# Rope scores of an attention stage on 64 array rows, four banks in one group per tile

## The chip, the core and the metric

One core of a Trainium2 chip runs the whole program. Its engines are TensorE (PE; its weight loads are listed as PEld), VectorE (DVE), ScalarE (ACT), GpSimd (POOL) and SyncE (SP), which here issues the DMAs. The metric is the device time of one execution in microseconds (us), the median of three. Times inside the program come from one profiled execution.

## The reference, cut to what matters

The program is one layer of an encoder: RMS norm and an input projection, an mLSTM head group, an attention head group, an output projection, a gated MLP and a gated per-layer embedding, on 2048 positions of width 1024. The change lies in the attention group (4 heads, 128 plain and 64 rope columns for each query and key) and at a few places before it:

```python
def mla_group(c_q, c_kv, k_rope_pre, q_norm_g, w_uq, kv_norm_g, w_ukv, cos, sin):
    q = (rms_norm(c_q, q_norm_g) @ w_uq).reshape(bsz, s, MLA_HEADS, QK_NOPE + QK_ROPE)
    q_nope, q_rope = q[..., :QK_NOPE], q[..., QK_NOPE:]
    q_rope = apply_rope(q_rope, cos[:, None, :], sin[:, None, :])
...
    scale = (QK_NOPE + QK_ROPE) ** -0.5
...
    def attend(blk):
        qn, qr = blk
        sc = (jnp.einsum('bqhd,bkhd->bhqk', qn, k_nope)
              + jnp.einsum('bqhr,bkr->bhqk', qr, k_rope))
        pr = jax.nn.softmax(sc.astype(jnp.float32) * scale, axis=-1)
        return jnp.einsum('bhqk,bkhd->bqhd', pr.astype(v.dtype), v)
```

## The kernel before, in words

Products keep float32 accuracy by splitting each operand into a high part, rounded to the reduced format fp32r, and a low part, the rest (`split`, L120 and L123). A product is then three matmuls: low by high, high by low, high by high (`mm3`, L133).

`in_proj` projects 128 rows of x at a time. `ssq_x` squares a tile of x on ACT, adds on DVE and sums over partitions with two matmuls by a column of ones (L237); POOL takes the power that gives the row's norm factor. `rest` (the columns for gates, query, key and rope) uses that factor one step later. `q_up`, run as side work between matmuls of a later part of the projection, makes the queries: DVE forms four rope products from PSUM (L607 to L610), the rotated result is turned and split, and one DRAM tensor, `q_d`, takes the plain part and, in its second plane, the rope part: its high half in rows 0 to 63, its low half in rows 64 to 127. Rope keys are the same for all heads. `split_kr` holds them twice over, in rows 0 to 63 and 64 to 127: `kr2` is the high part, `krl` the low part.

The attention stage runs over 64 tiles (4 heads by 16 tiles of 128 queries). A tile's scores against 2048 keys fill four PSUM banks of 128 x 512, and there are four such banks, so a bank has to be read by the exponential of one tile before the next tile's matmuls may use it. `score_bank` makes one bank with five matmuls (L918 to L922); two of them carry the rope part, L919 (`qr` by `krl`) and L921 (`qr` by `kr2`), where the 128 rows of `qr` hold the high and the low part of the query. DVE then takes the bank's maximum (L923). `soft` takes the maximum of the four, and a second instruction multiplies it by minus the scale (L934, L935). `expo` exponentiates a bank on ACT with that bias, the scale, and the row's sum (L941); after the fourth bank DVE adds the sums and inverts them (L946, L947). `transp` transposes a bank of exponentials (L981) into one of two banks and splits it, high on ACT, low on DVE. `pv` multiplies by the values for a pair of tiles, half the keys at a time (L993, L994); after the second half ACT copies (L997), DVE adds (L998), and two DMAs store the result (L1000). Queries come a pair of tiles ahead: `load_q` by one DMA (L900), three tiles before they are used, and `split_q`.

The order in which a tile's steps are written is a string:

```python
        order = "s0 E1 . s1 E2 . . t0 . s2 . E3 . t1 . s3 . . X e0 t2 . . t3 V . .".split()
```

Here s is a score bank of the next tile, E and e exponentials (E of the current tile, e0 the first of the next), t a transposition of the current tile, X `soft`, V half a value product, and at each point a step of side work may go, which is the mLSTM stage. A planner at compile time then fixes the order on each engine from that order and its own estimate of when operands are ready; `keep_in_program_order` pins one instruction behind the one written before it on its engine. On the chip each engine works through its fixed order. The output sums (`osums`, DVE) prepare weights of the later output projection beside attention.

Of the kernel before, what the change touches and what calls it, by code (L numbers as in the profile page):

```python
# [60 lines left out]
class Block:  # L61
# [114 lines left out]
    def in_proj(self):  # L176
# [51 lines left out]
        def ssq_x(st, x_t):  # L228
# [5 lines left out]
            nc.vector.tensor_tensor(ss[:, 0:2], ss[:, 0:2], ss[:, 2:4], op=ALU.add)  # L234
            ps = self.pml.tile([P, 4], F32, name="ssp", tag="ml")
            for i in range(2):
                nc.tensor.matmul(ps, ss[:, i], ones, start=i == 0, stop=i == 1)  # L237
# [65 lines left out]
        for st in range(NT + LAG_X):  # L303
# [9 lines left out]
            if 0 <= st - 1 < NT:  # L313
                ssq_x(st - 1, xq.pop(st - 1))
            if 0 <= st - LAG_X < NT:
                nq[st - LAG_X] = rest(st - LAG_X)
            if 0 <= st - LAG_X - LAG_R < NT:
                turn_rest(st - LAG_X - LAG_R, nq.pop(st - LAG_X - LAG_R))
# [174 lines left out]
    def split_kr(self, raws):  # L493

        self.kr2, self.krl = [self.at(f"x{14 + i}", [P, S], F32R, f"kr{i}") for i in range(2)]
        for c in range(4):
            sl = slice(c * 512, (c + 1) * 512)
            self.split(raws[c // 2][:, (c % 2) * 512:(c % 2) * 512 + 512], self.kr2[:, sl], self.krl[:, sl])
# [68 lines left out]
    def q_up(self):  # L567
# [16 lines left out]
        for c in range(8):  # L584
# [12 lines left out]
            for t in range(2):  # L597
# [9 lines left out]
                nc.vector.tensor_tensor(tt[:, 0], x1, cos, op=ALU.mult)  # L607
                nc.vector.tensor_tensor(tt[:, 1], x2, sin, op=ALU.mult)
                nc.vector.tensor_tensor(tt[:, 2], x2, cos, op=ALU.mult)
                nc.vector.tensor_tensor(tt[:, 3], x1, sin, op=ALU.mult)  # L610
# [9 lines left out]
                nc.scalar.copy(o[:, 2 * t:2 * t + 2], ps)  # L620
# [270 lines left out]
    def attend_begin(self):  # L891
# [6 lines left out]
        def load_q(h, pr):  # L898
            q = self.at(f"w{4 - pr % 2}", [P, 2, 256], F32R, "q_t")
            nc.sync.dma_start(_f(q), self.q_d[h, pr])  # L900
            qv[h, pr] = q

        def split_q(h, pr):
# [4 lines left out]
            qv[h, pr] = qs[:, 0], qs[:, 1], q[:, 1]  # L908
# [4 lines left out]
        def score_bank(s, kb):  # L913
            h, qt = s.h, s.qt
            qh, ql, qr = [t[:, (qt % 2) * P:(qt % 2) * P + P] for t in qv[h, qt // 2]]
            ks = slice(kb * 512, (kb + 1) * 512)
            ps = self.bank()
            mm(ps, ql, kh[:, ks], start=True, stop=False)  # L918
            mm(ps, qr, self.krl[:, ks], start=False, stop=False)  # L919
            mm(ps, qh, kl[:, ks], start=False, stop=False)  # L920
            mm(ps, qr, self.kr2[:, ks], start=False, stop=False)  # L921
            mm(ps, qh, kh[:, ks], start=False, stop=True)  # L922
            nc.vector.tensor_reduce(s.mx[:, kb:kb + 1], ps, axis=AX.X, op=ALU.max)  # L923
            s.banks.append(ps)
# [7 lines left out]
        def soft(s):  # L932
            s.nm = self.stat(1, "nm")
            nc.vector.tensor_reduce(s.nm, s.mx, axis=AX.X, op=ALU.max)  # L934
# [1141 lines left out]
```

## Time and profile before

| what | us |
|---|---|
| runs | 2884.54, 2886.15, 2884.79 (median 2884.79) |
| profiled execution | 2882.77, of which its span 2881.0 |
| granted TensorE clock, mean | 0.999 of full speed |
| attention stage | from about 494 to about 1217 of the span |

A row of the groups gives line, engine, operation, tile names (out<-in), shapes and count, then busy us and the mean ns of one, then the idle time of the engine just before and what ended it. In the timeline a row gives start, duration, engine, line and what ran; a name ending in x4 merges four in a row. The duration of a matmul is its latency through a pipeline, so consecutive ones overlap and the distance between starts is what one costs.

### The profile page before, as it was taken

The page shows a single profiled execution, that of the slowest core. Times are in us where ns is not written, and L with a number is a line of the kernel's source. Part 1 is how long each engine was busy: PE and PEld are TensorE (multiplying, and loading weights), DVE is VectorE, ACT ScalarE, POOL GpSimd, SP SyncE. Part 2 cuts the span into 40 slices and gives each one's busy share as a digit, 9 for nine tenths or more (in the row PEclk, how much of TensorE's full clock was granted, in tenths as well). Part 3 has the DMA queues.
Part 4 walks back from the last instruction along what each step waited for, and adds up shares of the span by engine and source line. Part 5 has one row for each costly group of instructions (what it writes and reads, how often), then busy time and mean ns, then how long its engine had stood idle before and what let it go on. Part 6 is the DMA issues. An engine that isn't in the chain of part 4 may idle for free.

```text
span 2881.0 us, 40250 instructions
## 1 busy us (share of the span) xinstructions
PE 2848.1 (99%) x14110; PEld 2387.4 (83%) x14110; DVE 2044.2 (71%) x3790; ACT 1508.0 (52%) x3006; POOL 220.6 (8%) x331
## 2 busy tenths in 40 slices
PE   8999999999999999999999999999999999999998
PEld 7888888888888888788888888888888888888787
DVE  7521555877777777776777877867777867676777
ACT  7311544656666566655755555655556333254665
POOL 3100000000000010034300000000000000002012
PEclk9999999999999999999999999999999999999999
DMA  6512545653333333378845544657766767576864
GB/s 194 129 59 68 168 121 173 211 175 114 105 112 98 98 112 111 125 246 274 273 140 177 194 167 149 217 183 239 235 230 208 238 193 246 165 265 204 287 203 163
DMA packets 408314, 508.94 MB, mean 177 GB/s; under 512 B 34080, under 2 KB 271664, under 8 KB 408112
## 3 DMA queue, kind: packets, MB, share of 16 engines
q1 hardware_dynamic: 408112, 506.37, 55.0%
q8 instruction: 111, 1.82, 0.2%
q14 instruction: 91, 0.75, 0.1%
HBM read 324.16 MB, written 182.12 MB: 176 GB/s over the span
## 4 chain that ended last, share of the span: by engine, by line
PE 88%; DVE 4%; issue 2%; DMA 2%; ACT 2%; POOL 1%; SPq 0%; POOLq 0%; ACTq 0%; DVEq 0%
PE fy L1440 21%; PE fz L1440 14%; PE fx L1440 14%; PE bk L133 14%; PE ppv L993 3%; PE tb L981 3%; PE bk L918 2%; PE bk L922 2%; PE bk L920 2%; PE bk L919 2%; PE bk L921 2%; PE ppv L994 2%; PE fs L133 2%; PE gb L133 1%; PE mb L856 1%
## 5 line engine op out<-in xcount | busy, mean ns | idle before, releaser
L1440 PE MATMUL fz<-op,fw 128*128 128x512 f32 x1968 | 478.2, 391 | 3.5 <-ACT fw L120 3.0
L1440 PE MATMUL fx<-op,fw 128*128 128x512 f32 x1968 | 475.8, 390 | 0.0
L1440 PE MATMUL fy<-op,fw 128*128 128x512 f32 x1968 | 474.8, 390 | 0.0
L1440 PEld LDWEIGHTS fz<-op,fw 128*128 128x128 f32 x1968 | 367.1, 188 | 82.1 <-ACT fw L120 4.6
L1440 PEld LDWEIGHTS fy<-op,fw 128*128 128x128 f32 x1968 | 368.6, 188 | 76.7 <-ACT fy L1553 0.4
L1440 PEld LDWEIGHTS fx<-op,fw 128*128 128x128 f32 x1968 | 368.2, 188 | 76.0
L1440 PE MATMUL fy<-op,fwd 128*128 128x512 f32 (+1 forms) x984 | 238.0, 390 | 0.5 <-DVE uv L1425 0.5
L120 ACT CAST pt<-tb 128x512 fp32r<-128x512 f32 x256 | 147.4, 587 | 166.8 <-PE tb L981 165.9
L133 PE MATMUL bk<-wsp,xh 128*128 128x512 f32 (+1 forms) x768 | 234.3, 386 | 0.0
L1440 PEld LDWEIGHTS fy<-op,fwd 128*128 128x128 f32 x984 | 182.6, 188 | 38.4 <-DVE uv L1425 0.9
L923 DVE TENSOR_REDUCE mx<-bk 128x1 f32<-128x512 f32 x256 | 174.4, 683 | 42.5 <-PE bk L922 41.4
L123 DVE TENSOR_TENSOR pt<-tb,pt 128x512 fp32r<-128x512 f32 x256 | 174.0, 683 | 30.0 <-ACT pt L120 28.5
L941 ACT ACTIVATE pe<-bk,nm 128x512 f32<-128x512 f32 x256 | 174.8, 696 | 35.6 <-DVE nm L935 33.6
L993 PE MATMUL ppv<-pt,kv 128*128 128x512 f32 x512 | 188.9, 407 | 0.5 <-DVE pt L123 0.5
L133 PEld LDWEIGHTS bk<-wsp,xh 128*128 128x128 f32 x768 | 145.3, 189 | 25.2
L133 PE MATMUL bk<-wsp,xl 128*128 128x512 f32 (+1 forms) x384 | 150.6, 392 | 7.7 <-DVE xl L123 7.7
L133 PE MATMUL bk<-xh,wqk 128*128 128x512 f32 x480 | 157.1, 393 | 0.0
L981 PE MATMUL tb<-ident,pe 128*128 128x128 f32 x1024 | 150.8, 273 | 3.9 <-DVE pt L123 3.3
L994 PE MATMUL ppv<-pt,kv 128*128 128x256 f32 x512 | 145.0, 283 | 0.0
L981 PEld LDWEIGHTS tb<-ident,pe 128*128 128x128 f32 x1024 | 121.9, 140 | 24.6 <-DVE pt L123 6.3
L120 ACT CAST fw<-hraw 128x1024 fp32r<-128x1024 f32 (+1 forms) x72 | 70.2, 981 | 116.1 <-PE fx L1440 58.9
L120 ACT CAST op<-opr 128x512 fp32r<-128x512 f32 x165 | 96.3, 620 | 60.2 <-DMA opr<-tw_d 13.3
(366 smaller groups left out, 5172.7 us busy)
## 6 DMA issues: line engine op xcount, KB each, us to landing
fwr<-in_w_up SPq DMA_DIRECT2D x66, 512.0 KB, 5.1
fh<-h_d SPq DMA_DIRECT2D x48, 512.0 KB, 3.7
h_d<-fh SPq DMA_DIRECT2D x48, 512.0 KB, 4.5
s_d<-fwr SPq DMA_DIRECT2D x44, 512.0 KB, 2.9
fws<-s_d SPq DMA_DIRECT2D x44, 512.0 KB, 3.6
rw<-row_d SPq DMA_DIRECT2D x32, 512.0 KB, 5.4
tw_d<-tsum SPq DMA_DIRECT2D x60, 256.0 KB, 5.2
opr<-tw_d SPq DMA_DIRECT2D x60, 256.0 KB, 4.8
```

The lines of the kernel that those rows point to most:

```text
L120: nc.scalar.copy(hi, src)
L123: (sub or nc.vector).tensor_tensor(lo, src, _f(hi), op=ALU.subtract)
L133: mm = lambda *a, **k: self.nc.tensor.matmul(*a, **k, skip_group_check=more)
L918: mm(ps, ql, kh[:, ks], start=True, stop=False)
L919: mm(ps, qr, self.krl[:, ks], start=False, stop=False)
L920: mm(ps, qh, kl[:, ks], start=False, stop=False)
L923: nc.vector.tensor_reduce(s.mx[:, kb:kb + 1], ps, axis=AX.X, op=ALU.max)
L941: nc.scalar.activation(s.pe[:, kb % 2], s.banks[kb], AF.Exp, bias=s.nm, scale=ASCALE, accum_out=s.rs[:, kb:kb + 1])
L981: nc.tensor.transpose(t[:, j, :], s.p[kb][:, j * P:(j + 1) * P], self.ident)
L993: mm(w.ps, vh[:, ks], pts[kb][:, j], start=kt == 0, stop=False, skip_group_check=True)
L994: mm(w.ps[:, 0], vl[:, ks], pts[kb][:, j, 0], start=False, stop=kt == NT - 1, skip_group_check=True)
L1440: nc.tensor.matmul(out, a[:, k * P:(k + 1) * P], parts[lo][:, cols], start=first, stop=lo == 1 and k == last, skip_group_check=more)
```

## The change

The rope part by high parts (L921) is taken out of the banks' own steps. In the fourth score step, after its first matmul, four matmuls on 64 array rows follow one another, one for each bank: banks 0 and 2 on rows 0 to 63, banks 1 and 3 on rows 64 to 127. For the odd ones the high query part is loaded a second time, into rows 64 to 127 of a third plane of the query tile. The product of the query's low part with the key's high part moves into L919: rows 64 to 127 of `krl` now hold the key itself, rounded. The maxima of banks 0 to 2 are taken after the group. The scale goes into the queries where they are made, and the maximum comes out negated.

Beside this, `rowsum` and the end of the value product (`pv_end`) become steps of their own, later in the order and pinned; the row sums of x (`rms_x`) move behind `rest`; and the output sums are pinned in written order.

```diff
@@ -232,9 +232,14 @@
             nc.vector.tensor_tensor(ss[:, 0:2], ss[:, 0:2], ss[:, 2:4], op=ALU.add)
+            return ss
+
+        def rms_x(st, ss):
             ps = self.pml.tile([P, 4], F32, name="ssp", tag="ml")
             for i in range(2):
-                nc.tensor.matmul(ps, ss[:, i], ones, start=i == 0, stop=i == 1)
+                m = nc.tensor.matmul(ps, ss[:, i], ones, start=i == 0, stop=i == 1)
+                if i == 0:
+                    self.tc.keep_in_program_order(m)
             t = self.stat(1, "rsm")
@@ -310,10 +315,11 @@
                 split_x(st, xq[st])
-            if 0 <= st - 1 < NT:
-                ssq_x(st - 1, xq.pop(st - 1))
+            ss = ssq_x(st - 1, xq.pop(st - 1)) if 0 <= st - 1 < NT else None
             if 0 <= st - LAG_X < NT:
                 nq[st - LAG_X] = rest(st - LAG_X)
+            if ss is not None:
+                rms_x(st - 1, ss)
             if 0 <= st - LAG_X - LAG_R < NT:
@@ -495,7 +501,10 @@
             sl = slice(c * 512, (c + 1) * 512)
-            self.split(raws[c // 2][:, (c % 2) * 512:(c % 2) * 512 + 512], self.kr2[:, sl], self.krl[:, sl])
+            raw = raws[c // 2][:, (c % 2) * 512:(c % 2) * 512 + 512]
+            self.nc.scalar.copy(self.kr2[:, sl], raw)
+            self.nc.vector.tensor_tensor(self.krl[0:64, sl], raw[0:64], _f(self.kr2[0:64, sl]), op=ALU.subtract)
+            self.nc.vector.tensor_copy(self.krl[64:P, sl], raw[64:P])
 
@@ -604,10 +613,10 @@
                 ro = self.at("s2", [P, NH, 64], name="qro")
-                nc.vector.tensor_tensor(tt[:, 0], x1, cos, op=ALU.mult)
-                nc.vector.tensor_tensor(tt[:, 1], x2, sin, op=ALU.mult)
-                nc.vector.tensor_tensor(tt[:, 2], x2, cos, op=ALU.mult)
-                nc.vector.tensor_tensor(tt[:, 3], x1, sin, op=ALU.mult)
+                nc.vector.scalar_tensor_tensor(tt[:, 0], x1, ASCALE, cos, op0=ALU.mult, op1=ALU.mult)
+                nc.vector.scalar_tensor_tensor(tt[:, 1], x2, ASCALE, sin, op0=ALU.mult, op1=ALU.mult)
+                nc.vector.scalar_tensor_tensor(tt[:, 2], x2, ASCALE, cos, op0=ALU.mult, op1=ALU.mult)
+                nc.vector.scalar_tensor_tensor(tt[:, 3], x1, ASCALE, sin, op0=ALU.mult, op1=ALU.mult)
                 nc.vector.tensor_tensor(ro[:, :, 0:32], tt[:, 0], tt[:, 1], op=ALU.subtract)
@@ -617,7 +626,7 @@
                         self.mm3(ps[:, i], wq[kt][0][:, ws], wq[kt][1][:, ws], ch[:, kt, :], cl[:, kt, :], kt == 0, kt == 1)
-                nc.scalar.copy(o[:, 2 * t:2 * t + 2], ps)
+                nc.scalar.activation(o[:, 2 * t:2 * t + 2], ps, AF.Copy, scale=ASCALE)
                 yield
@@ -896,8 +905,9 @@
         def load_q(h, pr):
-            q = self.at(f"w{4 - pr % 2}", [P, 2, 256], F32R, "q_t")
-            nc.sync.dma_start(_f(q), self.q_d[h, pr])
+            q = self.at(f"w{4 - pr % 2}", [P, 3, 256], F32R, "q_t")
+            nc.sync.dma_start(_f(q[:, 0:2]), self.q_d[h, pr])
+            nc.sync.dma_start(_f(q[64:P, 2]), self.q_d[h, pr, 0:64, 1])
             qv[h, pr] = q
@@ -905,23 +915,31 @@
             self.split(_f(q[:, 0]), qs[:, 0], qs[:, 1])
-            qv[h, pr] = qs[:, 0], qs[:, 1], q[:, 1]
+            qv[h, pr] = qs[:, 0], qs[:, 1], q[:, 1], q[:, 2]
 
...
             h, qt = s.h, s.qt
-            qh, ql, qr = [t[:, (qt % 2) * P:(qt % 2) * P + P] for t in qv[h, qt // 2]]
+            qh, ql, qr, q2 = [t[:, (qt % 2) * P:(qt % 2) * P + P] for t in qv[h, qt // 2]]
             ks = slice(kb * 512, (kb + 1) * 512)
             ps = self.bank()
+            s.banks.append(ps)
             mm(ps, ql, kh[:, ks], start=True, stop=False)
+            if kb == 3:
+                for n in range(4):
+                    half = slice(n % 2 * 64, n % 2 * 64 + 64)
+                    m = mm(s.banks[n], (qr, q2)[n % 2][half], self.kr2[half, n * 512:n * 512 + 512],
+                           start=False, stop=n < 3)
+                    if n:
+                        self.tc.keep_in_program_order(m)
+                        nc.vector.tensor_reduce(s.mx[:, n - 1:n], s.banks[n - 1], axis=AX.X, op=ALU.max)
             mm(ps, qr, self.krl[:, ks], start=False, stop=False)
             mm(ps, qh, kl[:, ks], start=False, stop=False)
-            mm(ps, qr, self.kr2[:, ks], start=False, stop=False)
-            mm(ps, qh, kh[:, ks], start=False, stop=True)
-            nc.vector.tensor_reduce(s.mx[:, kb:kb + 1], ps, axis=AX.X, op=ALU.max)
-            s.banks.append(ps)
+            mm(ps, qh, kh[:, ks], start=False, stop=kb == 3)
+            if kb == 3:
+                nc.vector.tensor_reduce(s.mx[:, 3:4], ps, axis=AX.X, op=ALU.max)
 
@@ -931,22 +949,22 @@
             s.nm = self.stat(1, "nm")
-            nc.vector.tensor_reduce(s.nm, s.mx, axis=AX.X, op=ALU.max)
-            nc.vector.tensor_scalar(s.nm, s.nm, -ASCALE, None, op0=ALU.mult)
+            nc.vector.tensor_reduce(s.nm, s.mx, axis=AX.X, op=ALU.max, negate=True)
             s.rs = self.stat(4, "rs")
...
                 s.pe = self.at(next(prot), [P, 2, 512], name="pe")
-            nc.scalar.activation(s.pe[:, kb % 2], s.banks[kb], AF.Exp, bias=s.nm, scale=ASCALE,
+            nc.scalar.activation(s.pe[:, kb % 2], s.banks[kb], AF.Exp, bias=s.nm,
                                  accum_out=s.rs[:, kb:kb + 1])
             s.p.append(s.pe[:, kb % 2])
-            if kb == 3:
-                ri = rsums[:, s.qt * NH + s.h:s.qt * NH + s.h + 1]
-                nc.vector.tensor_reduce(ri, s.rs, axis=AX.X, op=ALU.add)
-                nc.vector.reciprocal(ri, ri)
-
-        self.steps = load_q, split_q, score_bank, start, soft, expo
+
+        def rowsum(s):
+            ri = rsums[:, s.qt * NH + s.h:s.qt * NH + s.h + 1]
+            self.tc.keep_in_program_order(nc.vector.tensor_reduce(ri, s.rs, axis=AX.X, op=ALU.add))
+            nc.vector.reciprocal(ri, ri)
+
+        self.steps = load_q, split_q, score_bank, start, soft, expo, rowsum
         load_q(0, 0)
@@ -965,7 +983,7 @@
         mm = nc.tensor.matmul
-        load_q, split_q, score_bank, start, soft, expo = self.steps
+        load_q, split_q, score_bank, start, soft, expo, rowsum = self.steps
         rsums = self.gt.rearrange("p a b -> p (a b)")
@@ -995,9 +1013,14 @@
                 nc.scalar.copy(rb, w.ps[:, 0].rearrange("p (a t) -> p a t", a=2))
-                nc.vector.tensor_tensor(rb, rb, w.ps[:, 1].rearrange("p (a t) -> p a t", a=2), op=ALU.add)
-                for i in range(2):
-                    nc.sync.dma_start(self.y_d[2 * pr + i, :, 4 + h, :], rb[:, i])
+                w.rb = rb
+
+        def pv_end(w):
+            rb = w.rb
+            a = nc.vector.tensor_tensor(rb, rb, w.ps[:, 1].rearrange("p (a t) -> p a t", a=2), op=ALU.add)
+            self.tc.keep_in_program_order(a)
+            for i in range(2):
+                nc.sync.dma_start(self.y_d[2 * w.pr + i, :, 4 + w.h, :], rb[:, i])
 
@@ -1024,7 +1047,7 @@
         cur, self.xop = self.first, {}
-        pts, pend = [], None
+        pts, pend, whole = [], None, None
         osums, o = self.osums(), Out(self)
@@ -1058,8 +1081,10 @@
                         transp(cur, int(op[1]), pts)
-                        if i > 5 and op == "t3":
-                            next(osums, None)
+                        if op == "t3":
+                            rowsum(cur)
+                            if i > 5:
+                                next(osums, None)
                     elif op == "X" and nxt:
@@ -1074,12 +1099,17 @@
                         pv(pend, 1)
+                        whole = pend
+                    if whole and op in ("s0", "E1"):
+                        pv_end(whole)
+                        whole = None
             if qt % 2:
...
         pv(pend, 1)
+        pv_end(pend)
         sums(1)
@@ -1121,8 +1151,11 @@
 
-        tt = self.nc.vector.tensor_tensor
         L, H = slice(0, SB), slice(SB, 2 * SB)
+
+        def tt(o, x, y, op):
+            self.tc.keep_in_program_order(self.nc.vector.tensor_tensor(o, x, y, op=op))
+
         for k in range(4):
```

## The prediction

> **What bounds the kernel now.** I read the page first (busy shares, then the chain of waits), then the windows, then who waited for whom, then the timeline of single instructions.
>
> ```profile
> span 2881.0 us, 40250 instructions
> PE 2848.1 (99%) x14110; PEld 2387.4 (83%) x14110; DVE 2044.2 (71%) x3790; ACT 1508.0 (52%) x3006; POOL 220.6 (8%) x331
> ...
> PE 88%; DVE 4%; issue 2%; DMA 2%; ACT 2%; POOL 1%; SPq 0%; POOLq 0%; ACTq 0%; DVEq 0%
> ```
>
> TensorE (PE) is busy for 99% of the span and carries 88% of the chain that ended last. So a change is worth what it takes from PE's stream of matmuls, and costs what it adds there, either as work or as a gap. In the windows (stretch, length, then the busy us of PE, PEld, DVE, ACT, POOL) the stage that the change touches looks the same:
>
> ```profile
> 0.00:290.00 290.00, 280.05 (x1319) 237.20 (x1320) 122.10 (x388) 96.71 (x202) 39.10 (x70) 1.00 0.42 114
> ...
> 700.00:900.00 200.00, 198.94 (x1225) 172.12 (x1224) 151.38 (x410) 125.03 (x356) 17.03 (x24) 1.00 0.34 105
> ```
>
> In 200 us of attention PE idles 1.06 us; VectorE (DVE) is at 76%, ScalarE (ACT) at 63%. What little PE waits for in the attention stage, and one wait in the first projection:
>
> ```profile
> PE tb L981 <- DVE pt L123: 3.3, 9, 1.1
> PE bk L918 <- ACT pe L941: 2.0, 5, 0.7
> ```
> ```profile
> L237 PE MATMUL ssp<-ones,x_ss 128*128 128x4 f32 x64 | 8.4, 237 | 2.3 <-DVE x_ss L234 2.3
> ```
>
> The first two rows are from the waits of PE between 516 and 1200 us (total, times, longest). The second is the one to remember: a tile's first score matmul (L918) waits for the exponential that frees its bank, 5 times, 2.0 us in all.
>
> A matmul's listed 0.39 us is latency, and its slot is the distance between starts:
>
> ```profile
> 1200.12 0.39 PE L920 MATMUL bk<-kv,q_s 128*128 128x512 f32 x1
> 1200.12 0.19 PEld L921 LDWEIGHTS bk<-kr,q_t 128*128 128x128 f32 x1
> ...
> 1200.34 0.39 PE L921 MATMUL bk<-kr,q_t 128*128 128x512 f32 x1
> ...
> 1200.57 0.40 PE L922 MATMUL bk<-kv,q_s 128*128 128x512 f32 x1
> ...
> 1200.81 0.60 PE L981 MATMUL tb<-ident,pe 128*128 128x128 f32 x4
> ...
> 1201.16 0.48 PE L918 MATMUL bk<-kv,q_s 128*128 128x512 f32 x1
> ...
> 1201.48 0.40 PE L919 MATMUL bk<-kr,q_t 128*128 128x512 f32 x1
> ```
>
> The slot is 0.23 us (1200.34 to 1200.57). The weights of L921 load while L920 streams, so loads cost nothing. Going into 128-row transposes costs nothing either (0.24). The first full matmul after them has a slot of 0.32: its successor's load could not start early, 0.09 more.
>
> **The change part by part.**
>
> *The rope group.* Per tile (64 tiles), four 128-row matmuls of L921, one in each bank, go: 4 x 0.23 = 0.92 us. In their place come four 64-row matmuls in one run, on alternate halves of the array and in four banks. If the halves run at once, two slots of streaming remain, 0.46 us. The other 128-row rope matmul (L919) stays, with new content in the lower half of `krl`. So the most that the change can save is 0.46 x 64 = 29.4 us.
>
> Against this stand two changes of the array's row form in each tile, 128 to 64 rows and back. No 64-row matmul exists in this trace, but two smaller forms do. The 32-row transpose:
>
> ```profile
> 284.61 0.39 PE L133 MATMUL bk<-xh,wqk 128*128 128x512 f32 x1
> 284.93 0.24 PE L350 MATMUL tb<-ident,cw 32*128 32x32 f32 x1
> 285.10 0.51 PE L133 MATMUL bk<-xh,wqk 128*128 128x512 f32 x1
> 285.44 0.39 PE L133 MATMUL bk<-xl,wqk 128*128 128x512 f32 x1
> ```
>
> Before it the slot is 0.32 where 0.23 is usual: 0.09 to go in, which 128-row transposes did not pay. On the way out, the first full matmul has 0.34, so 0.11 for a load with no cover. And the 44-row transposes later:
>
> ```profile
> 1299.51 0.44 PE L1159 MATMUL fs<-ident,fcwr 44*128 44x44 f32 x4
> ...
> 1299.57 0.26 PEld L1159 LDWEIGHTS fs<-ident,fcwr 44*128 44x128 f32 x3
> ...
> 1299.59 0.35 PE L1159 MATMUL fs<-ident,fcwr 44*128 44x44 f32 x3
> ...
> 1299.72 0.23 PE L1159 MATMUL fs<-ident,fcwr 44*128 44x44 f32 x1
> ...
> 1299.88 0.50 PE L1440 MATMUL fy<-op,fw 128*128 128x512 f32 x1
> ```
>
> They start 0.07 us apart (1299.59 to 1299.72 is two steps), and the full matmul comes 0.16 after the last: 0.09 more to go out. So the group costs 0.46 + 0.09 in + 0.09 out + 0.11 uncovered load after it = 0.75 us at least. At most 0.10 is added for an uncovered load of the group's first weights (the size of the one behind it) and 0.08 for the second half starting late (1299.51 to 1299.59): 0.93. I take 0.80, nearer the lower end, because the second load (1299.57) already starts while the first matmul is in flight. Gain 0.92 - 0.80 = 0.12 us a tile, 7.7 us; the bounds are 10.9 us of gain and 0.6 of loss. Outside these bounds are the two rivals below, no switch cost at all and no overlap at all.
>
> The Trainium skill, "TensorEngine Tiling (Array Packing)", Key Properties, says that changing the tiling mode, unlike changing tiles within one, drains the engine; the 0.32 us in place of 0.23 agrees. "TensorE: Matmul & The Clock Gate", Measured speedup vs the span model, has packed matmuls starting about 4 ns apart; no run here shows that yet. By it the 0.08 for the late half falls away, the upper end is 0.85 and the least gain an estimated 4.5 us.
>
> *The maxima.* Banks 0 to 2 are now complete only after the group, in the fourth score step, so their three reduces (L923) move from one after each bank to one burst. Four in a row then stand ahead of the first exponential:
>
> ```profile
> 804.41 0.40 PE L922 MATMUL bk<-kv,q_s 128*128 128x512 f32 x1
> ...
> 809.24 0.39 PE L918 MATMUL bk<-kv,q_s 128*128 128x512 f32 x1
> ```
> ```profile
> 804.91 0.68 DVE L923 TENSOR_REDUCE mx<-bk 128x1 f32<-128x512 f32 x1
> 805.50 0.42 DVE L123 TENSOR_TENSOR q_s<-q_t,q_s 128x256 fp32r<-128x256 f32 x1
> 805.84 0.15 DVE L934 TENSOR_REDUCE nm<-mx 128x1 f32<-128x4 f32 x1
> 805.90 0.69 DVE L123 TENSOR_TENSOR pt<-tb,pt 128x512 fp32r<-128x512 f32 x1
> 806.51 0.14 DVE L935 TENSOR_SCALAR nm<-nm 128x1 f32<-128x1 f32 x1
> ```
> ```profile
> 807.10 0.70 ACT L941 ACTIVATE pe<-bk,nm 128x512 f32<-128x512 f32 x1
> ```
>
> Now the last score matmul ends at 804.81, the first exponential starts 2.3 us later and ends at 807.80, and the next tile's L918 starts at 809.24: 1.44 us to spare. After: counted from the group's first start, its first bank is whole at about 0.5 and read at 0.6, four reduces at 0.59 apart (804.91 to 805.50) end near 3.0, the small reduce follows, and the exponential can start near 3.2. The first full matmul behind the group starts near 0.65 (two slots, the first load at most 0.10, 0.09 to go out), the second 0.34 later, the third 0.23 later, and that ends at 1.6. So the exponential comes 1.6 us behind the last score matmul, less than the 2.3 of now, if nothing is put between the reduces. The merged negation takes L935 away, and with it the 0.67 us that it stood behind L934 (805.84 to 806.51). So I cost the burst at nothing; its cover is the 1.44 us. Where that is gone, each us late is a us of PE:
>
> ```profile
> 1208.23 0.19 PEld L918 LDWEIGHTS bk<-kv,q_s 128*128 128x128 f32 x1 [0.46 <-ACT pe L941]
> ```
>
> *Waits moved on DVE.* `rowsum` goes from behind the fourth exponential to the tile's fourth transposes, the sum of the two value halves from the second half's end to the next tile's first steps, each pinned there.
>
> ```profile
> L998 DVE TENSOR_TENSOR ya<-ya,ppv 128x256 f32<-128x256 f32 x32 | 13.4, 419 | 17.8 <-ACT ya L997 17.7
> ...
> L946 DVE TENSOR_REDUCE gt<-rs 128x1 f32<-128x4 f32 x64 | 9.7, 152 | 23.2 <-ACT pe L941 22.8
> ```
>
> DVE stands idle 17.7 and 22.8 us in front of these. Queued behind them are the reduces and the splits of transposed scores, which PE waits for at most 3.3 us (first waits above); so DVE gets room, and PE gains between 0 and 3.3 us, of which I count nothing. The two stores of each pair go to the SyncE queue (SP) later by one tile step; their readers come at the end of attention.
>
> *The row sums of x.* Their matmuls move behind a whole tile of the projection, so DVE has that time to finish: the 2.3 us of idle at L237 go. Bounds 0 to 2.3; I take 2.3, since a tile of the projection is 24 matmuls, about 5 us.
>
> *Work that lies beside PE.*
>
> ```profile
> q_t<-q_d SPq DMA_DIRECT2D x32, 256.0 KB, 2.9
> ```
> ```profile
> L919 PE MATMUL bk<-kr,q_t x256: 388/394/483, 494.3 to 1212.9; 128*128 128x512 f32 x128
> ...
> L123 DVE TENSOR_TENSOR kr<-krr,kr x4: 682/686/692, 478.6 to 480.4; 128x512 fp32r<-128x512 f32 x4
> ```
> ```profile
> L868 DVE SCALAR_TENSOR_TENSOR hy<-mb,den,hy 128x128 f32<-128x128 f32 x64 | 19.4, 341 | 0.5
> ```
> ```profile
> L607 DVE TENSOR_TENSOR qtt<-qpr,qcs x16: 280/281/292, 328.1 to 466.8; 128x128 f32<-128x128 f32 x16
> ```
>
> A second load of 64 KB follows each of the 32 query loads on SP. It goes to the same buffer, so it waits for nothing new, and it is issued three tiles ahead; hidden, and 2.9 us if that cover were gone. The key split adds four copies on 64 partitions, at most 4 x 0.69 = 2.7 us of DVE near 480; its first reader starts at 494.3, so it is hidden. Scaling the rope products makes 64 products at most 341 ns instead of 281, 3.8 us of DVE between 328 and 467 us, where PE is the full engine; nothing. The exponentials lose only an operand. The output sums are only kept in order.
>
> **The sum.** It is made against the profiled execution's own 2882.8 us (span 2881.0 and 1.8 around it): 2882.8 - 7.7 - 2.3 = 2872.8. The median of the runs stands 2.0 above that execution, so I predict 2875 us, 0.34% less.
>
> **The rivals.**
>
> *The switches cost nothing.* The 0.09 and 0.11 us belong to transposes of small fp32 tiles, and PE loads 64-row weights ahead as it does others. The whole 29.4 us come, and 2.3: 2853. For it: the load under L920 above. Against it: both narrow forms paid.
>
> *The halves do not run at once* (the change doesn't do what it says). Streaming stays at 0.92 and the switches, 0.80 - 0.46 = 0.34, are added: 0.34 x 64 = 21.8, less 2.3: 2904. Nothing in the trace shows two matmuls at once; nothing speaks against it either.
>
> *The burst makes the exponential late.* If another DVE instruction of its size stands in each of the three gaps between the reduces, as L123 stands between L934 and L935 above, the four reduces take 7 x 0.6 = 4.2 us instead of 2.4 and the exponential starts 3.4 us after the last score matmul, 1.1 later than now. Where 1.44 us are to spare that costs nothing, where none are (1208.23) PE loses 1.1. Waits now occur in 5 of some 60 tiles; with one tile in four, since the room of the others shrinks to 0.3, the mean is 0.28 us a tile, 17.6 us: 2882.8 - 10.0 + 17.6 + 2.0 = 2892. It decides from a mean of 0.16 us a tile, where it has eaten the 10.0 us. For it: DVE at 76% and a fixed order on each engine. Against it: the 40 us of DVE idle that the moved waits set free.
>
> **How the numbers follow.** A measurement of this kernel tells about 0.2% (5.8 us) from no change, so the bounds are 2879 and 2890.5. Forecast: 0.46, with its own range of 2871 to 2884, of which 0.10 lies above 2879. No switch cost: 0.16. No overlap: 0.14. Late exponential: 0.24, of which 0.07 ends within 0.2%. Faster 0.36 + 0.16 = 0.52, same 0.17, slower 0.17 + 0.14 = 0.31. The range goes from 2853 to 2899 and leaves out the case without overlap and the tail of the late one, under 0.2.
>
> **What would show it.** Rows of form 64*128 in pairs that start under 0.1 us apart, the second pair 0.23 later, show the overlap; starts 0.23 apart each show its absence. The slot before the group (0.32 or 0.23) and the distance from its last start to the next full matmul show the switches; from the start of the full matmul ahead of the group to that of the second one behind it I expect 0.23 + 0.80 + 0.23 = 1.26 us, where 1.38 would be no gain. PE's wait for ACT at a tile's first score matmul tells of the burst: 2 us in all as now, or 18. The 2.3 us at the ones-matmul should be gone. The forecast is wrong if the group takes 0.92 or more, or if that wait passes 12 us.

## The result, and the profile after

The changed kernel takes 2893.4 us (median of six runs, 2891.67 to 2894.89), the kernel before 2884.66 in the same comparison: a ratio of 1.0027, 95% interval 1.0017 to 1.0038. It is slower by 0.3%. Its profiled execution took 2891.67 us. Two executions of the kernel before, run beside the experiments, took over 5800 us and count in no median here. The page of the changed kernel, the span, the busy times and the chain by engine:

```profile
span 2889.9 us, 40244 instructions
PE 2850.8 (99%) x14110; PEld 2362.0 (82%) x14110; DVE 2027.5 (70%) x3730; ACT 1506.9 (52%) x3006; POOL 215.1 (7%) x331
...
PE 92%; DVE 3%; ACT 2%; DMA 1%; issue 1%; POOL 1%; POOLq 0%; SPq 0%; ACTq 0%; DVEq 0%
```

The shares say almost nothing: PE is at 99% as before, and DVE and ACT are less busy than they were. The windows of the changed kernel, the two shown of before and one over most of the attention stage:

```profile
0.00:290.00 290.00, 280.86 (x1326) 238.81 (x1327) 123.08 (x389) 96.34 (x205) 39.10 (x70) 1.00 0.42 116
...
516.00:1200.00 684.00, 673.63 (x4105) 553.50 (x4104) 503.17 (x1307) 417.69 (x1139) 44.24 (x64) 1.00 0.42 129
700.00:900.00 200.00, 197.76 (x1209) 162.74 (x1207) 150.63 (x396) 122.56 (x349) 17.43 (x24) 1.00 0.43 134
```

The same window of the kernel before:

```profile
516.00:1200.00 684.00, 676.32 (x4135) 583.51 (x4134) 528.70 (x1380) 421.81 (x1148) 46.16 (x64) 1.00 0.40 126
```

In equal time PE got through 4105 matmuls instead of 4135, and it idled 10.4 us (684.00 - 673.63) instead of 7.7. The waits of PE in that window of the changed kernel (total, times, longest), and the ones-matmul from its groups:

```profile
PE mb L894 <- DVE hy L889: 4.5, 5, 1.2
PE bk L929 <- ACT pe L958: 4.2, 7, 1.4
PE tb L999 <- DVE pt L123: 0.8, 2, 0.4
```
```profile
L240 PE MATMUL ssp<-ones,x_ss 128*128 128x4 f32 x64 | 8.2, 234 | 1.5 <-DVE x_ss L234 1.5
```

Two waits have grown: a tile's first score matmul for the exponential (2.0 to 4.2), and that of the transposes of `hy`, which belong to the mLSTM stage, the side work between a tile's steps (1.2 to 4.5). The second one in the kernel before:

```profile
PE mb L885 <- DVE hy L880: 1.2, 2, 0.9
```

Attention now lasts 741.3 us from its first score matmul to the start of its last value matmul, and lasted 732.3. It begins 1.7 us earlier (492.4 against 494.1), and the stretch behind it is 1.6 us longer, where the traces of all kernels here lie 6.9 us apart. So the loss is in attention. What stands open in the waits is too little to explain it, because a matmul is listed with 0.39 us where its slot is 0.23: a delay below the difference shows as busy. The distances between starts show all of it. In this table each PE instruction of the stage is charged the distance from the start of the one before it to its own start, summed in us; "first" is the first score matmul of each tile from the second on, "hy" are the 64 mLSTM transposes of `hy`, "scores" the other 1216 score matmuls, and "rest" everything else. The kernels e1 to e15 are the experiments below; each has one profiled execution, which lies up to 5.7 us from the median of its runs (e11), so a difference of a few us between two rows isn't a finding by itself.

| kernel | stage | first | hy | scores | rest |
|---|---|---|---|---|---|
| before | 732.3 | 9.4 | 11.7 | 267.1 | 444.1 |
| after | 741.3 | 13.6 | 16.1 | 264.0 | 447.6 |
| e3 | 725.9 | 5.6 | 9.8 | 266.2 | 444.3 |
| e1 | 743.0 | 15.3 | 17.0 | 263.5 | 447.1 |
| e4 | 741.1 | 15.3 | 17.0 | 265.7 | 443.1 |
| e12 | 749.5 | 23.3 | 13.9 | 266.0 | 446.3 |
| e11 | 749.0 | 5.3 | 11.1 | 288.8 | 443.8 |
| e6 | 764.0 | 13.4 | 16.5 | 291.7 | 442.3 |
| e8 | 734.8 | 6.8 | 11.3 | 266.7 | 450.0 |
| e13 | 728.4 | 5.7 | 9.7 | 266.5 | 446.5 |
| e14 | 726.0 | 5.7 | 10.7 | 260.9 | 448.8 |
| e15 | 726.7 | 5.9 | 11.0 | 271.4 | 438.5 |

The changed kernel wins 3.1 us in the score matmuls and loses 4.2 at the tiles' first ones, 4.4 at `hy` and 3.5 elsewhere.

**The group.** From the timeline of the changed kernel (start, duration, engine, line, what ran), a whole group, and its first two matmuls apart from the next two:

```profile
814.03 0.48 PE L929 MATMUL bk<-kv,q_s 128*128 128x512 f32 x1
814.44 0.73 PE L933 MATMUL bk<-kr,q_t 64*128 64x512 f32 x4
815.10 0.50 PE L938 MATMUL bk<-kr,q_t 128*128 128x512 f32 x1
815.43 0.40 PE L939 MATMUL bk<-kv,q_s 128*128 128x512 f32 x1
815.67 0.40 PE L940 MATMUL bk<-kv,q_s 128*128 128x512 f32 x1
```
```profile
814.44 0.50 PE L933 MATMUL bk<-kr,q_t 64*128 64x512 f32 x2
```

Two last as long as one alone (0.50), so the halves run at once, and four are through in 0.66 (814.44 to 815.10). Going in, the slot of L929 is 0.41 where 0.32 is usual behind transposes; coming out, that of L938 is 0.33 where 0.23 is usual. So the group costs 0.66 + 0.09 + 0.10 = 0.85 us in place of 0.92.

In 10 of the 64 tiles the planner put other work between the group's first matmul, which isn't pinned, and the other three, so that the row form changes four times:

```profile
882.96 0.50 PE L933 MATMUL bk<-kr,q_t 64*128 64x512 f32 x1
883.39 0.71 PE L780 MATMUL mb<-v,kk 128*128 128x129 f32 x4
884.04 0.73 PE L933 MATMUL bk<-kr,q_t 64*128 64x512 f32 x3
884.70 0.50 PE L938 MATMUL bk<-kr,q_t 128*128 128x512 f32 x1
```

**The burst.** The tile of the prediction's timeline, in the changed kernel: last score matmul, DVE's work, first exponential, next tile's first score matmul.

```profile
804.71 0.40 PE L940 MATMUL bk<-kv,q_s 128*128 128x512 f32 x1
...
809.54 0.39 PE L929 MATMUL bk<-kv,q_s 128*128 128x512 f32 x1
```
```profile
804.01 0.69 DVE L937 TENSOR_REDUCE mx<-bk 128x1 f32<-128x512 f32 x1 [0.22 <-PE bk L933]
804.62 0.68 DVE L123 TENSOR_TENSOR pt<-tb,pt 128x512 fp32r<-128x512 f32 x1
805.22 0.68 DVE L937 TENSOR_REDUCE mx<-bk 128x1 f32<-128x512 f32 x1
805.82 0.41 DVE L123 TENSOR_TENSOR q_s<-q_t,q_s 128x256 fp32r<-128x256 f32 x1
806.15 0.69 DVE L937 TENSOR_REDUCE mx<-bk 128x1 f32<-128x512 f32 x1
806.75 0.68 DVE L942 TENSOR_REDUCE mx<-bk 128x1 f32<-128x512 f32 x1
807.35 0.68 DVE L123 TENSOR_TENSOR pt<-tb,pt 128x512 fp32r<-128x512 f32 x1
807.94 0.15 DVE L952 TENSOR_REDUCE nm<-mx 128x1 f32<-128x4 f32 x1
```
```profile
808.13 0.69 ACT L958 ACTIVATE pe<-bk,nm 128x512 f32<-128x512 f32 x1 [0.62 <-DVE nm L952]
```

Two splits stand between the reduces and a third ahead of the small one (L952). The exponential starts 3.0 us behind the end of the last score matmul (805.11), and its end leaves 0.72 us until 809.54; before it was 2.3 and 1.44. Over 61 tiles the medians are 3.00 and 0.66 us, and were 2.63 and 1.02.

How the late exponential reaches `hy` is seen in another tile of the changed kernel's timeline: ACT, then DVE, then PE.

```profile
1119.56 0.69 ACT L958 ACTIVATE pe<-bk,nm 128x512 f32<-128x512 f32 x1 [0.68 <-DVE nm L952]
...
1120.24 0.30 ACT L886 ACTIVATE hy<-hy 128x128 f32<-128x128 f32 x1
...
1121.12 0.30 ACT L886 ACTIVATE hy<-hy 128x128 f32<-128x128 f32 x1
```
```profile
1122.92 0.88 DVE L889 SCALAR_TENSOR_TENSOR hy<-hy,rsr,og 128x128 f32<-128x128 f32 x3 [1.51 <-POOL rsr L143]
```
```profile
1123.33 0.33 PE L894 MATMUL mb<-ident,hy 128*128 128x128 f32 x1 [1.03 <-DVE hy L889]
```

ACT idles 0.68 us until the maximum is there. The mLSTM stage's four squares (L886) stand behind that exponential in ACT's order; POOL takes the power of their sums, DVE waits 1.51 us for it, and PE 1.03 us for DVE.

### The profile page after: what moved, and what is told of

The parts are those of the page before. It is cut to its first block, busy times and chain, and to the rows that moved or that the text cites. A ratio compares the mean times of both kernels' runs of the same rounds, so it can differ in the third digit from the quotient of the medians.

```text
span 2889.9 us, 40244 instructions
## 1 busy us (share of the span) xinstructions
PE 2850.8 (99%) x14110; PEld 2362.0 (82%) x14110; DVE 2027.5 (70%) x3730; ACT 1506.9 (52%) x3006; POOL 215.1 (7%) x331
## 4 chain that ended last, share of the span: by engine, by line
PE 92%; DVE 3%; ACT 2%; DMA 1%; issue 1%; POOL 1%; POOLq 0%; SPq 0%; ACTq 0%; DVEq 0%
PE fy L1473 22%; PE fz L1473 15%; PE fx L1473 15%; PE bk L133 14%; PE ppv L1011 3%; PE tb L999 3%; PE bk L938 2%; PE bk L929 2%; PE bk L940 2%; PE bk L939 2%; PE ppv L1012 2%; PE fs L133 2%; PE gb L133 1%; PE bk L933 1%; PE mb L865 1%; PE mb L866 1%
## 5 line engine op out<-in xcount | busy, mean ns | idle before, releaser
L999 PEld LDWEIGHTS tb<-ident,pe 128*128 128x128 f32 x1024 | 122.7, 141 | 22.7 <-ACT pe L958 2.4
L937 DVE TENSOR_REDUCE mx<-bk 128x1 f32<-128x512 f32 x192 | 126.7, 683 | 18.1 <-PE bk L933 18.0
```

What stands on the lines that cost most here:

```text
L937: nc.vector.tensor_reduce(s.mx[:, n - 1:n], s.banks[n - 1], axis=AX.X, op=ALU.max)
L999: nc.tensor.transpose(t[:, j, :], s.p[kb][:, j * P:(j + 1) * P], self.ident)
```

## The experiments

Times are given as the difference of medians to the runs of the kernel before on the same chip, with the ratio's 95% interval.

| kernel | edit in short | median us | minus before | ratio |
|---|---|---|---|---|
| e1 | after, the group's first matmul pinned too | 2893.8 | +8.8 | 1.0022 to 1.0045 |
| e2 | e1 without the moved work | 2900.42 | +15.4 | 1.0039 to 1.0065 |
| e3 | before, with all but the group | 2878.44 | -6.6 | 0.9971 to 0.9989 |
| e4 | e1, group on 128 rows | 2892.08 | +7.0 | 1.0014 to 1.0035 |
| e5 | e1, group opens its step | 2890.85 | +7.2 | 1.0013 to 1.0030 |
| e8 | e1, maxima of banks 0 to 2 early | 2886.65 | +3.0 | 1.0003 to 1.0021 |
| e9 | e8 and e5 together | 2892.84 | +9.2 | 1.0020 to 1.0044 |
| e10 | e8 on 128 rows | 2885.78 | +2.1 | 0.9996 to 1.0014 |
| e6 | e1, all four on one half | 2916.74 | +31.7 | 1.0093 to 1.0125 |
| e11 | e1, two groups of two | 2898.5 | +13.4 | 1.0034 to 1.0060 |
| e12 | e3 with late reduces | 2901.21 | +16.1 | 1.0038 to 1.0064 |
| e13 | before, with scaling only | 2880.72 | -4.4 | 0.9976 to 0.9993 |
| e14 | e8, group three matmuls later | 2879.17 | -4.7 | 0.9975 to 0.9993 |
| e15 | e14 on 128 rows | 2879.75 | -4.1 | 0.9977 to 0.9995 |

**Which part loses: e1, e2, e3, e4.** e1 pins the first matmul of the group as well:

```diff
-                    if n:
-                        self.tc.keep_in_program_order(m)
+                    self.tc.keep_in_program_order(m)
+                    if n:
```

e2 is e1 with `rowsum`, the end of the value product and the row sums of x back where they were, and the output sums unpinned. e3 is the kernel before with these moves, the scaled queries and the negated maximum, and neither group nor burst. e4 is e1 with the group's place and burst, but four matmuls on all 128 rows:

```diff
-                    m = mm(s.banks[n], (qr, q2)[n % 2][half], self.kr2[half, n * 512:n * 512 + 512],
+                    m = mm(s.banks[n], qr, self.kr2[:, n * 512:n * 512 + 512],
```

> The changed kernel with the first of the four 64-row matmuls pinned too. In the changed kernel's trace that first one runs apart from the other three in 10 of 64 tiles, and each of these pays a second change of row form: 0.09 in, 0.10 for an uncovered load, 0.23 of a stream that overlaps nothing, 0.09 out, 0.10 behind, about 0.6 us. Theory A (the change of row form is the loss): all 64 groups whole, 6 us less than the changed kernel, about 2887. Theory B (the burst of reduces makes PE wait): 2893 as before, since the burst stays. Theory C (the moved and pinned DVE work makes the waits): 2893 too.

> The kernel e1_pin0 with the moved work put back: row sums of x at once, row sums of the exponentials and the end of the value product where they were, output sums free. Theory A: as e1_pin0 plus the 1.7 us that the row sums of x saved, about 2889. Theory C (the moved and pinned DVE work costs): less than e1_pin0 by 4 us or more. Theory B: PE's waits for exponentials grow, since DVE stands before row sums and value sums again; 2892 or more.

> The kernel before with only the moved and pinned work, the scaled queries and the negated maximum; scores as before, five 128-row matmuls a bank, a reduce after each. Theories A and B: the moved work costs nothing, 1.7 us less than before by the row sums of x, about 2883. Theory C: slower than before, 2888 or more.

> The kernel e1_pin0 with the group's four matmuls on 128 rows (query parts by high keys as before the change), at the same place, with the same pins and the same burst of reduces. The group costs 4 x 0.23 = 0.92 instead of 0.86 a tile. Theory A: 0.06 x 64 = 4 us more than e1_pin0, about 2891. Theory B: the burst is the loss with any rows, so it stays 6 us or more above the kernel before, 2891 or more, as much as e1_pin0 does plus 4. Were the 64-row form worth its full 29 us, this would be 29 above e1_pin0.

In e1 58 of the 64 groups are whole, where after has 54. The other six still have side work behind the group's first matmul, though each of the four is pinned: a pin keeps two instructions in order, it doesn't keep others out. So e1 tests theory A on four groups only, 2.4 us by its own 0.6 each. It stands at +8.8 where after has +8.7, and its two waits, same window, are no shorter:

```profile
PE bk L929 <- ACT pe L958: 5.6, 9, 1.4
PE mb L894 <- DVE hy L889: 5.5, 7, 1.3
```

e2 is 6.6 us slower than e1, so the moved work isn't what loses. e3, expected at 2883, takes 2878.4 and beats both kernels. e4, with 128 rows and no change of form, loses as much as e1, with the same two waits:

```profile
PE bk L926 <- ACT pe L954: 5.7, 8, 1.4
PE mb L891 <- DVE hy L886: 5.6, 6, 1.3
```

From e3 to e4 the stage grows by 15.2 us: 9.7 at the first score matmuls, 7.2 at `hy`, and 1.7 less elsewhere. So the loss belongs to the order of matmuls and reduces, not to the row form.

**Is it the burst: e8, e10, e5, e9.** e8 is e1 with the maxima of banks 0 to 2 taken early, before the product of the high rope parts is in them:

```diff
-                    if n:
-                        nc.vector.tensor_reduce(s.mx[:, n - 1:n], s.banks[n - 1], axis=AX.X, op=ALU.max)
...
-            mm(ps, qh, kh[:, ks], start=False, stop=kb == 3)
-            if kb == 3:
-                nc.vector.tensor_reduce(s.mx[:, 3:4], ps, axis=AX.X, op=ALU.max)
+            mm(ps, qh, kh[:, ks], start=False, stop=True)
+            nc.vector.tensor_reduce(s.mx[:, kb:kb + 1], ps, axis=AX.X, op=ALU.max)
```

e10 is the same on 128 rows. e5 keeps the burst and puts the group ahead of bank 3's own matmuls; e9 does both.

> The kernel e1_pin0 with the maximum of banks 0 to 2 taken where it was before the change, after each bank's own three remaining matmuls, so without the product of the high rope parts; bank 3's is whole. Any shift gives the same softmax, as long as the exponential stays in range: here the missing part moves a row's maximum by at most 73. The group of 64-row matmuls stays. Theory B (the burst of reduces is the loss): PE's waits fall to those of e3_extras_only, 2878.4, and the group saves 0.06 x 64 = 4 us of that: about 2875. Theory A (the 64-row form, or its place, is the loss): no less than 2890.

> The kernel e4_fullrows (the group on 128 rows) with the maximum of banks 0 to 2 taken early, without the product of the high rope parts, as in e8_partial. The same matmuls as e3_extras_only, four of them moved into one run, and no burst. Theory B: 2878, as e3_extras_only, 14 us less than e4_fullrows; e8_partial lies 4 us below it. Rival (moving the matmuls together makes the waits, whatever DVE does): 2890 or more.

> The kernel e1_pin0 with the group ahead of the fourth bank's own matmuls instead of behind the first of them (the group's last matmul opens bank 3). The group then follows transposes, behind which the first weight load is uncovered anyway, so one of the three uncovered loads of 0.10 goes: 6 us of PE. The reduces begin 0.3 us earlier. Theory B: the burst stays, so most of the waits stay: 2885 to 2888. If the change of row form were the loss, 2888 with no change in the waits.

> e8_partial with the group ahead of the fourth bank's own matmuls, as in e5_first: 64-row form, no burst, one uncovered load less. Theory B: 6 us less than e8_partial, about 2869, under both kernels. Rival (uncovered loads are not what they seem, the next matmul pays in any case): as e8_partial.

e8 wins back 5.8 of the 8.8 us and misses its 2875. The exponential now starts 1.42 us behind the last score matmul (median), and "first" and "hy" fall to 6.8 and 11.3. There is a new wait: the group's third matmul writes bank 2, which its reduce is still reading.

```profile
PE bk L925 <- DVE mx L940: 3.0, 7, 0.7
```

And the planner breaks 28 of e8's 64 groups in two with side work, so that the row form changes four times in these tiles. e10 tells the same of the burst on 128 rows: it misses its 2878, with the same new wait (3.1 us), but stands 4.9 us nearer to the kernel before than e4. e5 stands 1.6 below e1, inside the intervals, and above its expectation; its two waits are no shorter (6.7 and 5.3). e9 missed its expectation: half of its groups are broken, and 4.6 us of waiting for `hy` came back, while the wait for the reduce of bank 2 is shorter than in e8 (1.5). Why it gives up all of e8's gain isn't settled.

**The burst alone, and the small parts: e12, e13.** e12 is e3, where each bank keeps its own five matmuls, and the reduces of banks 0 to 2 only have to wait for bank 3's first matmul:

```diff
             m = mm(ps, ql, kh[:, ks], start=True, stop=False)
+            if kb == 3:
+                for n in range(3):
+                    r = nc.vector.tensor_reduce(s.mx[:, n:n + 1], s.banks[n], axis=AX.X, op=ALU.max)
+                    self.tc.add_manual_dep(r.ins, m.ins.name, mybir.DependencyInfo(
+                        mybir.DependencyClass.Sync, mybir.DependencyReason.DATA), reason="burst")
```

e13 is the kernel before with the scaled queries and the negated maximum alone.

> The kernel e3_extras_only with the reduces of banks 0 to 2 made to wait for the first matmul of the fourth bank. Matmuls, their form and their written order stay; only the burst is added, and nothing on PE waits for the reduces themselves. Theory B (the burst is the loss): the exponentials start 0.7 us later after the last score matmul, PE's waits grow as in e4_fullrows, 2889 to 2893. Rival (the four matmuls moved into one run make the waits): 2878, as e3_extras_only.

> The kernel before with the scaled queries and the negated maximum alone; no work moved or pinned, scores as before. e3_extras_only is 6.6 us under the kernel before. If the removed multiplication (L935, which stood 0.67 us behind the reduce before it) is the gain: about 2880. If the moved and pinned DVE work is: 2884, as before.

e12 loses 22.7 us to e3 with not one matmul altered. In the stage 17.7 us come at the first score matmuls and 4.1 at `hy`. Its burst begins some 0.45 us later than e4's, which can account for the larger loss. The planner also set side work at other places than in e3, so it isn't the burst wholly alone. Its first wait:

```profile
PE bk L925 <- ACT pe L952: 10.8, 17, 1.4
```

The scaling with the negation is worth 4.4 us (e13): "first" falls from 9.4 to 5.7 and "hy" from 11.7 to 9.7. e3, with the moved work too, stands another 2.2 lower, inside the intervals. How the gain comes about can be seen in e3's timeline: last score matmul, DVE, first exponential.

```profile
800.31 0.40 PE L928 MATMUL bk<-kv,q_s 128*128 128x512 f32 x1
...
800.80 0.68 DVE L929 TENSOR_REDUCE mx<-bk 128x1 f32<-128x512 f32 x1
801.40 0.41 DVE L123 TENSOR_TENSOR q_s<-q_t,q_s 128x256 fp32r<-128x256 f32 x1
801.73 0.15 DVE L940 TENSOR_REDUCE nm<-mx 128x1 f32<-128x4 f32 x1
...
801.91 0.69 ACT L946 ACTIVATE pe<-bk,nm 128x512 f32<-128x512 f32 x1
```

No split can come between the small reduce and the exponential any more, which starts 1.2 us behind the last score matmul in this tile, 2.12 in the median (2.20 in e13) where before has 2.63.

**The price of the row form: e6, e11, e14, e15.** e6 puts all four matmuls of e1's group on rows 0 to 63. e11 makes two groups of two, in the second and the fourth step, so the reduces spread again and the form changes twice as often. e14 and e15 are e8 and e10 with the group behind three of bank 3's own matmuls, to let the reduce of bank 2 finish first:

```diff
             mm(ps, ql, kh[:, ks], start=True, stop=False)
+            mm(ps, qr, self.krl[:, ks], start=False, stop=False)
+            mm(ps, qh, kl[:, ks], start=False, stop=False)
             if kb == 3:
...
-            mm(ps, qr, self.krl[:, ks], start=False, stop=False)
-            mm(ps, qh, kl[:, ks], start=False, stop=False)
             mm(ps, qh, kh[:, ks], start=False, stop=True)
```

> The kernel e1_pin0 with all four matmuls of the group on rows 0 to 63, so that no two can run at once; otherwise the same. If the halves overlap in e1_pin0, two more slots of 0.23 a tile: 29 us more, about 2923. If they do not overlap there, no change, 2894.

> The kernel e1_pin0 with two groups a tile: banks 0 and 1 in the second score step, banks 2 and 3 in the fourth. Each group of two costs 0.09 in, 0.10 for the first load, 0.23 of streaming, 0.09 out, 0.10 for the load behind, 0.61 us, so 1.22 a tile instead of 0.86: 23 us more than e1_pin0 by theory A, 2917. Theory B takes some 5 us off that, since half of the burst goes: 2912. If the change of row form were free, this would lie under e1_pin0 by what the burst cost.

> The kernel e8_partial with the group three matmuls into the fourth bank instead of one, so that the early maximum of bank 2 is done when the group writes that bank; again the maxima of banks 0 to 2 are taken without the product of the high rope parts. In e8_partial PE waited 3.0 us for that reduce in the open, and its groups were 5 us longer in all than in e1_pin0. With neither burst nor that wait only the 64-row form itself is left. Theory: its saving is 0.06 x 64 = 4 us at the most, 2875 to 2879, under the kernel before. Rival (the group costs in its own right): 2884 or more.

> The kernel e10_full_partial with the group at the same later place, on 128 rows. Its matmuls are those of e3_extras_only (2878.4), so 2878 to 2881 if burst and wait were all that stood against the group; e14_partial_late lies 0 to 4 us below it, which is what the 64-row form is worth. Rival: e14_partial_late lies above it.

The rows of the group from the groups by line (busy, mean ns, idle), e1 and then e6:

```profile
L933 PE MATMUL bk<-kr,q_t 64*128 64x512 f32 x256 | 49.9, 447 | 0.0
```
```profile
L932 PE MATMUL bk<-kr,q_t 64*128 64x512 f32 x256 | 78.1, 420 | 0.0
```

Without the second half the group is busy 28.2 us longer, 0.44 a tile, which is two slots. In time e6 stands 22.9 above e1 where 29 were expected, since "first" and "rest" fall by 6.7. In e11 "first" and "hy" are at the level of e3, but the score matmuls take 25.3 us more than in e1, 0.40 for each further visit to the narrow form. e11 was expected at 2912 or more and took 2898.5: spreading the reduces over two groups takes away nearly all of the burst's loss, not 5 us of it.

e14 came out 0.2 us above its range and e15 inside its own. But the wait for the reduce of bank 2 stays, 2.6 us in e14 and 2.7 in e15; other waits fell, that of the transposes for DVE from 2.0 in e8 to 0.5 in e14, and 17 groups are broken instead of 28. Which of these made the 7.7 us from e8 to e14 isn't settled.

e14 and e15 differ by 0.6 us in time. The 64-row group saves 10.5 us in the score matmuls, and the work between takes 10.3 more: 6.7 of that at the first instruction behind a tile's scores, 0.338 us from the start before it where e15 has 0.234, and 4.3 at side work inside broken groups. One of these, in e14:

```profile
572.06 0.50 PE L925 MATMUL bk<-kr,q_t 64*128 64x512 f32 x2
572.49 0.71 PE L780 MATMUL mb<-v,kk 128*128 128x129 f32 x4
573.13 0.49 PE L925 MATMUL bk<-kr,q_t 64*128 64x512 f32 x2
573.56 0.51 PE L925 MATMUL bk<-kv,q_s 128*128 128x512 f32 x1
```

In e14 and e15 PE works through the same instructions in the same order, and so it does in e1 and e4. That allows a comparison tile by tile, from the start of bank 3's first matmul to the start of the first instruction behind the tile's scores:

| 64 rows against 128 | whole groups, median of one | broken groups, median of one | all whole | all broken |
|---|---|---|---|---|
| e1 against e4 | -0.058 us (58 tiles) | +0.48 us (6 tiles) | -3.3 us | +2.9 us |
| e14 against e15 | -0.061 us (47 tiles) | +0.29 us (17 tiles) | -2.7 us | +3.4 us |

So the narrow form does gain, 0.06 us in each whole group as e4's expectation had it, and the broken groups lose it again. With all 64 whole it would be worth an estimated 3.8 us (0.06 x 64). A kernel with whole groups and no burst wasn't run. As they ran, e14 and e15 stand 1.9 and 2.5 us above e3, with overlapping intervals.

## Why the prediction was wrong, by its own steps

**The step that failed** is "So I cost the burst at nothing". It rests on an exponential 1.6 us behind the last score matmul, "if nothing is put between the reduces". Something was: the exponential came 3.0 us behind, the cover of 1.44 us shrank to 0.72 in that tile, and where it was gone PE waited. The quoted rows of before had already shown a split between the two small instructions, so the undisturbed count of 2.4 us for four reduces was the less likely one. The price: e4 against e3, 13.6 us; the changed kernel against e3, 15.3 (8.7 + 6.6).

**The rival** "the burst makes the exponential late" (2892, chance 0.24) was the case by its own mechanism. Its sum came near in part by luck: of the 10.0 us that it takes off, 7.7 were for a group that gave less, and the 6.6 of the small edits (e3) stood in their place. It put all 17.6 us at the first score matmul. The runs showed a second place: from e3 to the changed kernel the stage grew by 15.4, of which 8.0 at the first score matmuls and 6.3 at the `hy` transposes. The prediction asked which bank waits for the exponential, and not what is queued behind it on ACT: the squares of the mLSTM stage. Its test, that wait passing 12 us, did not fire, with 4.2 us: about half of the 8.0 is in pieces that a matmul's listed latency covers, and the rest of the loss is at `hy`. Its other test, a group of 0.92 or more, did not fire either (0.85).

**The group** was off in size. Overlap, price of the way in (0.09) and out, and the bounds (0.75 to 0.93) held; 0.85 was measured in place of 0.80, since the next load did not start early behind a change of form. The loads behind the group of 814.44:

```profile
815.10 0.19 PEld L938 LDWEIGHTS bk<-kr,q_t 128*128 128x128 f32 x1 [0.36 <-issue]
815.21 0.19 PEld L939 LDWEIGHTS bk<-kv,q_s 128*128 128x128 f32 x1
815.44 0.19 PEld L940 LDWEIGHTS bk<-kv,q_s 128*128 128x128 f32 x1
```

That of L939 starts 0.11 us behind L938 (815.10), that of L940 with L939 (815.43). Inside the group the second pair stands 0.33 us behind the first, 0.10 over a slot; the prediction had taken most of that load as covered. What is left, 0.07 a tile, is 4.5 us instead of 7.7. And the prediction did not foresee broken groups: by the figures of e1 (0.058 and 0.48, so this is an estimate) the 54 whole ones of the changed kernel win 3.1 us, and the ten broken ones lose 4.8. The mark of 1.26 us for a gain and 1.38 for none was misplaced: measured were 1.40 (814.03 to 815.43), but the matmul ahead of the group stands behind transposes, where the slot is 0.32, so 1.47 would be no gain. In time nothing was seen of the form: e4 stands 1.8 below e1, e15 0.6 above e14.

**No overlap** is refuted by the pairs and by e6. **Switches that cost nothing** are refuted by the group's rows and by e11.

**The row sums of x**: 2.3 us predicted, and attention began 1.7 earlier. In the traces with the moved sums it begins between 491.5 and 492.9, in the three without (before, e2, e13) between 494.1 and 495.7, so the size is about right. But 1.5 us of idle at the ones-matmul remain, so not all of it went there.

**The small edits counted at nothing** were worth the most. The negation that left DVE's chain served the prediction only as cover for the burst; by itself it and the scaled queries are worth 4.4 us (e13). The moved work, row sums of x included, is worth 2.2 more beside them, which the intervals don't tell from nothing, and 6.6 beside the burst (e2 against e1). The second query loads lie beside PE as predicted: e1, which has them, shows no wait of PE for them in the stage. For the scaled products it is open: e13, which has them without the moved sums, begins attention 1.6 us later than before.

The best version that computes all that the reference does is e3, 0.2% below the kernel before (0.9971 to 0.9989).

## What to carry to other kernels

Before reads on one engine are gathered behind a later event, follow the chain from that event to the next use of the buffer with the neighbours that the engine's order already shows in between, and compare it with the spare time of each round; busy shares of 70% and 52% hid a loss of 15 us here. Ask what else is queued behind the late instruction, on its engine and the next, since side work is late too. Look in the trace whether instructions that were to stand together do, since pins alone left up to half of the groups broken. And try the small edits that come with a large one alone: here they were the gain.

## What the runs showed of the hardware

Two 64-row matmuls on different halves of the array start 3 to 4 ns apart in the trace (median 3) and last as long as one. A visit to the narrow form costs about 0.4 us beyond its streaming (0.40 in e11, and 0.85 - 0.46 = 0.39 in the group above), nearly the two slots (0.46) that four matmuls save: 0.06 us a group remain, and one interruption costs several times that. And 2.7 us more of visible idle stood for a stage that was 9.0 us longer: with a listed latency of 0.39 us and a slot of 0.23, only the distances between starts show what is lost.
